# A decoder layer on one core: the order of the first loads, of the first two tiles' norms, and of the bias product

## The chip, the cores and the metric

The kernel runs on one core of one Trainium2 chip. The metric is the device time of that core for one execution, in microseconds (us). The engines are TensorE (PE; its weight loads are listed as PEld), VectorE (DVE), ScalarE (ACT), GpSimd (POOL) and SyncE (SP), whose queue issues nearly all transfers.

## The reference

One layer of a hybrid decoder, 512 positions by 1024 channels, float32:

```python
h = rms_norm(x, g_pre_mix)
q, k, v, xr, gr = split(h @ w_in)
attn = moba_attention(q, k, v, rel_bias)          # 8 heads of 64, blocks of 256, T5 bias
xr   = causal_dwconv(xr, w_conv_lru, b_conv_lru)  # width 4
lru  = rg_lru(xr, w_r, b_r, w_i, b_i, lam) * gelu(gr)
x    = x + rms_norm(concat(attn, lru) @ w_out, g_post_mix)
h    = rms_norm(x, g_pre_ffn)
c_u, c_g = split(causal_dwconv(h @ w_up, w_conv_ffn, b_conv_ffn))   # width 3, 2 x 2816
x    = x + rms_norm((gelu(c_g) * c_u) @ w_down, g_post_ffn)
```

## The kernel before

Positions are cut into four tiles of 128 rows. Every product of two float32 matrices is made from rounded parts: a high part (the value rounded to the PE's faster float32 form) and a low part (the rest), and three products high by high, low by high and high by low. So each operand is first copied by ScalarE (high) and then subtracted by VectorE or GpSimd (low).

The opening is written out by hand: from the first load to the end of the recurrent group's gates, PE, ScalarE, VectorE and SP each run in the order in which the lines stand (a block `manual_schedule`); behind it a planner orders the work, and POOL's order is the planner's throughout. What stands in the opening:

- Loads on SP: x tile 0 in two halves, x tile 1, then `load_xr(0)`, the first 128 columns of the weights for `xr` (512 KB, like a tile of x); then eight small loads of parameters into `rows` (L219 to L225); then x tile 2, `load_xr(1)`, x tile 3, `load_xr(2)`, `load_xr(3)` (L227 to L231), and four loads of the gate weights into `graw`. The scale of the norm, the one-hot table and the relative bias come on ScalarE's queue.
- Three warming products of PE (`keep_warm`, on constants, their result is not used), then `gpre`, the norm's scale spread over all rows by a product with ones, and `pfb` (L261), the product of the bias table with the one-hot table.
- Per tile of x: `sums` (ScalarE, squares with their sum), `rstd` (the root on ScalarE, some small operations on VectorE), `norm(t, half)` (VectorE), `turn(t, half)` (four PE transposes of 128 columns into one PSUM bank), `upper` (ScalarE copies the high part out) and `lower` (VectorE makes the low part).
- Per block of `xr` weights: `xr_upper(t)` (ScalarE's rounded copy) and `xr_lower(t, eng)` (the low part, on GpSimd for blocks 0 and 2, on VectorE for 1 and 3).
- `px_products(t, ...)`, the products of block t with half of the positions: C0 is the first two tiles, C1 the last two; 24 products each. The bank `p_x[t]` then goes to the conv (`conv_first` on ScalarE, `conv_rest` on VectorE), which needs `par`: the parameters in `rows`, transposed by two PE transposes into `ppar` and copied out by VectorE.
- Behind C1 come block 3 (`px3`), the gates (`gates(t)`, which read `xs`, the high and low part of the conv's result), the products for v and for g, and attention.
- `fb` is the scaled bias (L320, ScalarE, from `pfb`), stored to DRAM as `fbd` (L321), spread to `toep` by a transfer (L553) and read back by attention's `tb` loads.

PSUM banks are taken by tag: `mm` 3, `sc` 2, `tr` 2, `av` 1; a new tile of a tag waits for the readers of the one that had its bank.

Of the kernel before, what the change touches and what calls it, by code (L numbers as in the profile page):

```python
# [19 lines left out]
S = 512  # L20
D = 1024
H = 8
# [17 lines left out]
ISCALE = DH ** -0.5  # L40
# [12 lines left out]
def hybrid_layer(  # L53
# [6 lines left out]
    nc = tc.nc  # L60
# [9 lines left out]
    def bank(name, tag):  # L70
        return ps.tile([P, 512], F32, tag=tag, name=name, bufs=BANKS[tag])

    def f32(ap):
        return ap.bitcast(F32)


    def mm3(o, lhs, rhs, start, stop):
        (lh, ll), (rh, rl) = lhs, rhs
        nc.tensor.matmul(o, lh, rh, start=start, stop=False)  # L79
        nc.tensor.matmul(o, lh, rl, start=False, stop=False)  # L80
        nc.tensor.matmul(o, ll, rh, start=False, stop=stop)  # L81
# [5 lines left out]
    def load_raw(src, k, n):  # L87
        t = wp.tile([P, k, n], F32, tag="raw", name="raw", bufs=2)
        nc.sync.dma_start(t, src.rearrange("(k p) n -> p k n", p=P))
        return t  # L90
# [7 lines left out]
    def at(hl, *idx):  # L98
        return hl[0][idx], hl[1][idx]


    xres = cp.tile([P, NT, D], F32, name="xres")
    x_v = x.rearrange("(t p) d -> p t d", p=P)
# [7 lines left out]
    oh, rb = bias_in[:, :S], bias_in[:, S:S + H]  # L111
# [19 lines left out]
    def rstd_of(ss, first, name):  # L131


        v = cp.tile([P, 5], F32, tag="rs", name=name, bufs=8)
        nc.scalar.activation(v[:, 0:1], ss, AF.Sqrt, scale=1.0 / D, bias=first[:, 0:1])
        nc.vector.tensor_scalar(
            v[:, 1:2], ss, -0.5 / D, first[:, 1:2], op0=ALU.mult, op1=ALU.add)
        nc.vector.reciprocal(v[:, 2:3], v[:, 0:1])
        nc.vector.scalar_tensor_tensor(
            v[:, 3:4], v[:, 2:3], v[:, 1:2], v[:, 2:3], op0=ALU.mult, op1=ALU.mult)  # L140
        nc.vector.scalar_tensor_tensor(
            v[:, 4:5], v[:, 3:4], 1.5, v[:, 2:3], op0=ALU.add, op1=ALU.mult)
        return v[:, 4:5]
# [9 lines left out]
    def normalised(hn, t, r, gn, hs):  # L153
        nc.vector.scalar_tensor_tensor(
            hn[:, hs], xres[:, t, hs], r, gn, op0=ALU.mult, op1=ALU.mult)

    def transposes(hn, half, pt):
        for j in range(4):
            k = 4 * half + j
            nc.tensor.transpose(pt[:, j * P:(j + 1) * P], hn[:, k * P:(k + 1) * P], ident)  # L160

    def part(t, half):
        return slice(None), slice(4 * half, 4 * half + 4), slice(t * P, (t + 1) * P)

    def by_rows(pt):
        return pt.rearrange("p (k q) -> p k q", q=P)
# [31 lines left out]
    def xr_cols(t):  # L198
        return raw_xr[t // 2][:, :, (t % 2) * P:(t % 2 + 1) * P]

    def load_xr(t):
        nc.sync.dma_start(xr_cols(t), w_xr[:, :, t * P:(t + 1) * P])
# [8 lines left out]
    fb = gp.tile([H, FE], F32, name="fb")  # L211
# [4 lines left out]


    rows = pp.tile([P, 2, P], F32, name="rows")
    for r0, src in ((0, w_conv_lru[0]), (16, b_conv_lru), (20, b_r), (24, b_i), (28, lam)):  # L219
        v = src.rearrange("a (t c) -> (a t) c", c=P)  # L220
        nc.sync.dma_start(rows[r0:r0 + v.shape[0], 0], v)
# [1 line left out]
    wcf = w_conv_ffn[0].rearrange("a (t c) -> (a t) c", c=P)  # L223
    nc.sync.dma_start(rows[76:80, 0], wcf[P:P + 4])
    nc.sync.dma_start(rows[:, 1], wcf[0:P])  # L225

    nc.sync.dma_start(xres[:, 2], x_v[:, 2])  # L227
    load_xr(1)
    nc.sync.dma_start(xres[:, 3], x_v[:, 3])
    load_xr(2)  # L230
    load_xr(3)  # L231
    nc.gpsimd.memset(graw, 0.0)
    for g, w in enumerate((w_r[0], w_i[0])):
        wv = w.rearrange("(t b) c d -> b c t d", b=2)
# [6 lines left out]
    fbd = dp.tile([H, FE], F32, name="fbd")  # L241
# [7 lines left out]
    def keep_warm(n):  # L249

        for _ in range(n):
            nc.tensor.matmul(pwarm, warm[:, 0:P], warm, start=True, stop=True)
# [4 lines left out]
    gpre = [bank(f"gpre{n}", "sc") for n in range(2)]  # L257
    for n in range(2):
        nc.tensor.matmul(gpre[n], ones, g_row[:, n * 512:(n + 1) * 512], start=True, stop=True)
    pfb = bank("pfb", "av")  # L260
    nc.tensor.matmul(pfb[0:H, :], rb, oh, start=True, stop=True)  # L261


    hn, ssn, rn, pt = {}, {}, {}, {}
# [1 line left out]
    def sums(t, parts):  # L266
        hn[t] = pp.tile([P, D], F32, tag="hn", name="hn", bufs=4)
        ssn[t] = cp.tile([P, 4], F32, tag="ss", name="ss", bufs=8)
        square(t, ssn[t], parts, pp)

    def rstd(t, parts):
        ss = ssn[t]
        if parts == 2:
            for i, f in ((2, 1.0), (3, -0.5)):
                nc.vector.tensor_scalar(
                    ss[:, i:i + 1], ss[:, 0:1], f / D, f * EPS, op0=ALU.mult, op1=ALU.add)
            rn[t] = rstd_of(ss[:, 1:2], ss[:, 2:4], "rpre")
        else:
            rn[t] = rstd_of(ss[:, 0:1], consts, "rpre")

    def norm(t, half):
        normalised(hn[t], t, rn[t], gpre[half], slice(512 * half, 512 * half + 512))

    def turn(t, half, tag):
        pt[t, half] = bank("ptr", tag)
        transposes(hn[t], half, pt[t, half])

    def upper(t, half):
        nc.scalar.copy(hT[0][part(t, half)], by_rows(pt[t, half]))

    def lower(t, half):
        sl = part(t, half)
        nc.vector.tensor_sub(hT[1][sl], by_rows(pt[t, half]), f32(hT[0][sl]))
# [3 lines left out]
    def xr_upper(t):  # L297
        w_x[t] = [wp.tile([P, KD, P], F32R, tag=f"w{i}", name=f"w{i}") for i in "hl"]
        nc.scalar.copy(w_x[t][0], xr_cols(t))

    def xr_lower(t, eng):
        eng.tensor_sub(w_x[t][1], xr_cols(t), f32(w_x[t][0]))

    HH, HL, LH = range(3)
    BY_KIND = [(k, i) for i in (HH, HL, LH) for k in range(KD)]

    def px_products(t, c0, c1, todo, first, last):

        cs = slice(c0, c1)
        for n, (k, i) in enumerate(todo):  # L310
            nc.tensor.matmul(p_x[t][:, cs], w_x[t][i == LH][:, k], hT[i == HL][:, k, cs],  # L311
                             start=first and n == 0, stop=last and n == len(todo) - 1)

    C0, C1 = (0, S // 2), (S // 2, S)
    sums(0, 2)
    rstd(0, 2)
    sums(1, 1)
    norm(0, 0)
    rstd(1, 1)
    nc.scalar.mul(fb[:, 0:S], pfb[0:H, :], 1.0 / ISCALE)  # L320
    nc.sync.dma_start(fbd, fb)  # L321
    turn(0, 0, "tr")
    norm(1, 0)
    norm(0, 1)
    upper(0, 0)
    lower(0, 0)
    xr_upper(0)
    xr_lower(0, nc.gpsimd)
    turn(1, 0, "tr")
    upper(1, 0)  # L330
    turn(0, 1, "mm")
    upper(0, 1)
    norm(1, 1)
    lower(1, 0)
    lower(0, 1)
    p_x[0] = bank("px", "mm")
    px_products(0, *C0, [(k, HH) for k in range(4)], True, False)
    turn(1, 1, "av")
    upper(1, 1)
    lower(1, 1)  # L340
    px_products(0, *C0, [(k, HL) for k in range(4)] + [(k, HH) for k in range(4, 8)]
                + [(k, LH) for k in range(4)] + [(k, HL) for k in range(4, 8)]
                + [(k, LH) for k in range(4, 8)], False, True)
# [7 lines left out]
    px_products(1, *C0, BY_KIND, True, True)  # L351
    sums(3, 1)
    rstd(3, 1)
    turn(2, 0, "tr")
    turn(2, 1, "tr")
    upper(2, 0)
    upper(2, 1)
    norm(3, 0)
    norm(3, 1)
    xr_upper(2)  # L360
    xr_lower(2, nc.gpsimd)
    lower(2, 0)
    lower(2, 1)
    p_x[2] = bank("px", "mm")
# [4 lines left out]
    upper(3, 1)  # L369
    lower(3, 0)  # L370
    lower(3, 1)
    ppar = bank("ppar", "av")
    nc.tensor.transpose(ppar[:, 0:80], rows[0:80, 0], ident[0:80, 0:80])
    nc.tensor.transpose(ppar[:, 80:80 + P], rows[:, 1], ident)
    nc.vector.tensor_copy(par, ppar[:, 0:80 + P])
    for t in range(3):
        px_products(t, *C1, BY_KIND, True, True)
    xr_upper(3)
    xr_lower(3, nc.vector)

    def w_conv_l(tap, t):
        return par[:, 4 * tap + t:4 * tap + t + 1]
# [24 lines left out]
    av = lp.tile([P, NT, S], F32, name="av")  # L407
# [4 lines left out]
    def conv_first(t):  # L412
        nc.scalar.activation(xc[:, t], p_x[t], AF.Identity, scale=w_conv_l(3, t), bias=col(16 + t))

    def conv_rest(t):
        for d in range(1, 4):
            nc.vector.scalar_tensor_tensor(
                xc[:, t, d:], p_x[t][:, :S - d], w_conv_l(3 - d, t), xc[:, t, d:],
                op0=ALU.mult, op1=ALU.add)

    def xs_upper(t):
        xs[t] = [lp.tile([P, S], F32R, tag=f"xs{i}", name=f"xs{i}") for i in "hl"]
        nc.scalar.copy(xs[t][0], xc[:, t])
# [38 lines left out]
    def v_products(u, j):  # L462
        if u == 0 and j == 0:
            p_v.extend(bank(f"pv{t}", ("tr", "tr", "av", "mm")[t]) for t in range(NT))
        k = 2 * u + j
        for t in range(NT):
            mm3(p_v[t], at(hT, slice(None), k, slice(t * P, (t + 1) * P)),
                at(w_v[u], slice(None), j), k == 0, k == KD - 1)
# [11 lines left out]
    def gr_split(t):  # L480
        if t % 2 == 0:
            raw_gr.append(load_raw(w_in[:, GR0 + t * P:GR0 + t * P + 256], KD, 256))
        w_gr.append(split_w(raw_gr[-1][:, :, (t % 2) * P:(t % 2 + 1) * P], KD, P))
# [26 lines left out]
    nc.vector.tensor_sub(gw[1], graw, f32(gw[0]))  # L510
    conv_first(1)
    xs_upper(0)
    conv_rest(1)
    xs_lower(0)
    conv_first(2)
# [26 lines left out]
    gates(3)  # L542
    decay(2)
    gr_split(0)
    v_products(2, 1)
    sigmoids(3)
    gr_split(1)
# [349 lines left out]
```

## Time and profile before

| what | value |
|---|---|
| median of 3 runs | 589.23 us (588.77 to 589.48) |
| profiled execution, its own time | 588.1 us |
| its span, first to last instruction | 586.1 us |
| PE busy | 572.9 us (98%), 2731 products and transposes |
| PE weight loads | 472.4 us (81%) |
| VectorE, ScalarE, GpSimd busy | 358.4, 279.1, 15.5 us |
| transfers | 59.62 MB, mean 102 GB/s |

A product's row in the trace runs from its start to a modelled end, so rows of one engine overlap, and a full PE is not a PE at its peak. A row's last bracket gives the idle time of its engine just ahead of it and what ended that. Times are counted from the span's start.

### The profile page before, as it was taken

The numbers are of one execution on the slowest core, as the hardware profiler recorded it, in microseconds if no ns is written. First come the engines' busy times: TensorE is split into PE (matmuls) and PEld (weight loads), VectorE is DVE, ScalarE is ACT, GpSimd is POOL, SyncE is SP. The second block draws the span as 40 slices with busy tenths as digits, with TensorE's granted clock in tenths as the row PEclk, the third lists the DMA queues.
The fourth block names the chain that finished last, engine by engine and source line by source line (L and its number), as shares of the span: only waits on it lengthen the run. The fifth ranks groups of instructions, "written<-read, shape, count | busy, mean of one in ns | idle before, by whom it ended". The sixth has DMA issues, their size and how long they took to land.

```text
span 586.1 us, 7041 instructions
## 1 busy us (share of the span) xinstructions
PE 572.9 (98%) x2731; PEld 472.4 (81%) x2731; DVE 358.4 (61%) x649; ACT 279.1 (48%) x457; POOL 15.5 (3%) x37
## 2 busy tenths in 40 slices
PE   8899999999999999999999999999999999999995
PEld 4798888777778879988888888888888888888884
DVE  5687787898896895656656656656656521241225
ACT  6458856778775662534443443444444322132121
POOL 2150000000000000000000000000000000000000
PEclk9999999999999999999999999999999999999998
DMA  7824535333201614003413412412414223232103
GB/s 222 240 73 134 170 91 161 127 108 108 73 1 45 217 64 144 1 28 117 144 41 103 143 51 94 145 62 82 143 69 141 78 72 107 92 126 72 37 0 143
DMA packets 53449, 59.62 MB, mean 102 GB/s; under 512 B 2480, under 2 KB 42624, under 8 KB 53417
## 3 DMA queue, kind: packets, MB, share of 16 engines
q1 hardware_dynamic: 53319, 59.11, 31.3%
q8 instruction: 21, 0.34, 0.2%
q14 instruction: 11, 0.09, 0.1%
q10 hardware_dynamic: 98, 0.07, 0.0%
HBM read 57.06 MB, written 3.69 MB: 104 GB/s over the span
## 4 chain that ended last, share of the span: by engine, by line
PE 88%; DVE 4%; ACT 4%; DMA 2%; issue 1%; POOL 0%; SPq 0%; DVEq 0%; ACTq 0%
PE pup L80 14%; PE pup L81 14%; PE pup L79 14%; PE py L81 8%; PE py L79 8%; PE py L80 8%; PE px L311 2%; PE pq L79 2%; PE pq L80 2%; PE pq L81 2%; PE pav L661 2%; PE ptp L651 1%; PE pv L80 1%; PE pv L79 1%; PE pgr L80 1%; PE pgr L79 1%
## 5 line engine op out<-in xcount | busy, mean ns | idle before, releaser
L85 DVE TENSOR_TENSOR wl<-raw,wh 128x1024 fp32r<-128x1024 f32 x78 | 95.3, 1222 | 125.7 <-ACT wh L84 125.4
L84 ACT CAST wh<-raw 128x1024 fp32r<-128x1024 f32 x78 | 81.7, 1049 | 140.1 <-PE py L81 72.2
L81 PE MATMUL pup<-h2Th,wl 128*128 128x512 f32 x320 | 124.5, 389 | 0.0
L80 PE MATMUL pup<-h2Tl,wh 128*128 128x512 f32 x320 | 124.5, 389 | 0.0
L79 PE MATMUL pup<-h2Th,wh 128*128 128x512 f32 x320 | 124.3, 389 | 0.0
L81 PEld LDWEIGHTS pup<-h2Th,wl 128*128 128x128 f32 x320 | 60.1, 188 | 12.5
L80 PEld LDWEIGHTS pup<-h2Tl,wh 128*128 128x128 f32 x320 | 60.1, 188 | 12.5
L79 PEld LDWEIGHTS pup<-h2Th,wh 128*128 128x128 f32 x320 | 60.0, 188 | 12.3
L79 PE MATMUL py<-wh,acth 128*128 128x512 f32 x176 | 68.9, 391 | 0.0
L81 PE MATMUL py<-wh,actl 128*128 128x512 f32 x176 | 68.8, 391 | 0.0
L80 PE MATMUL py<-wl,acth 128*128 128x512 f32 x176 | 68.8, 391 | 0.0
L81 PEld LDWEIGHTS py<-wh,actl 128*128 128x128 f32 x176 | 33.1, 188 | 7.3
L80 PEld LDWEIGHTS py<-wl,acth 128*128 128x128 f32 x176 | 33.1, 188 | 7.2
L79 PEld LDWEIGHTS py<-wh,acth 128*128 128x128 f32 x176 | 33.1, 188 | 7.1
L819 DVE SCALAR_TENSOR_TENSOR yu<-pup,par,yu 128x511 f32<-128x511 f32 (+1 forms) x44 | 33.0, 749 | 4.3 <-ACT yu L817 3.6
L826 ACT ACTIVATE yg<-yg 128x512 f32<-128x512 f32 x22 | 13.9, 632 | 44.7 <-DVE yg L819 44.7
L819 DVE SCALAR_TENSOR_TENSOR yg<-pup,par,yg 128x511 f32<-128x511 f32 (+1 forms) x44 | 32.8, 746 | 2.0 <-ACT yg L817 1.2
L827 DVE TENSOR_TENSOR yu<-yu,yg 128x512 f32<-128x512 f32 x22 | 15.3, 693 | 18.0 <-ACT yg L826 18.0
L81 PE MATMUL py<-wh,mixTl 128*128 128x512 f32 x64 | 25.4, 397 | 0.0
L79 PE MATMUL pq<-hTh,wh 128*128 128x512 f32 x64 | 25.4, 396 | 0.0
L81 PE MATMUL pq<-hTh,wl 128*128 128x512 f32 x64 | 25.3, 396 | 0.0
L79 PE MATMUL py<-wh,mixTh 128*128 128x512 f32 x64 | 25.3, 395 | 0.0
(213 smaller groups left out, 934.4 us busy)
## 6 DMA issues: line engine op xcount, KB each, us to landing
raw<-in_w_up_dram SPq DMA_DIRECT2D x22, 1024.0 KB, 5.0
raw<-in_w_down_dram SPq DMA_DIRECT2D x10, 1024.0 KB, 5.0
raw<-in_w_in_dram SPq DMA_DIRECT2D x4, 1024.0 KB, 5.2
rawqk<-in_w_in_dram SPq DMA_DIRECT2D x8, 512.0 KB
raw<-in_w_out_dram SPq DMA_DIRECT2D x4, 1024.0 KB
raw<-in_w_in_dram SPq DMA_DIRECT2D x4, 512.0 KB
out_dram<-yz SPq DMA_DIRECT2D x8, 256.0 KB, 2.1
xres<-in_x_dram SPq DMA_DIRECT2D x3, 512.0 KB, 3.8
```

The costliest lines, as they stand in the source:

```text
L79: nc.tensor.matmul(o, lh, rh, start=start, stop=False)
L80: nc.tensor.matmul(o, lh, rl, start=False, stop=False)
L81: nc.tensor.matmul(o, ll, rh, start=False, stop=stop)
L84: nc.scalar.copy(h, src)
L85: (sub or nc.vector).tensor_sub(l, src, f32(h))
L311: nc.tensor.matmul(p_x[t][:, cs], w_x[t][i == LH][:, k], hT[i == HL][:, k, cs], start=first and n == 0, stop=last and n == len(todo) - 1)
L651: nc.tensor.transpose(ptr[:, j * P:(j + 1) * P], st[:, j * P:(j + 1) * P], ident)
L661: nc.tensor.matmul(pav[:, j * P:], vs, pT[i][:, j * S:j * (S - P) + S], start=j == 0 and i == 0, stop=j == NT - 1 and i == 1)
L819: nc.vector.scalar_tensor_tensor(y[:, d:], pt[:, :S - d], w_conv_f(2 - d, blk), y[:, d:], op0=ALU.mult, op1=ALU.add)
L826: nc.scalar.activation(yg, yg, AF.Gelu_apprx_tanh)
L827: nc.vector.tensor_mul(yu, yu, yg)
```

## The change

Parts of the opening change places; no arithmetic changes, and three warming products are added.

- SP: x tile 2, `load_xr(1)`, x tile 3, `load_xr(2)` and `load_xr(3)` go ahead of the eight loads of parameters. The store of `fb` moves behind `gr_split(0)`.
- PE: `pfb` leaves the start for a place between `px_products(1)` and `px_products(2)` of C1, and takes a bank of tag `sc`, where it had one of `av`; one warming product stands at its old place and two behind `turn(0, 0)`. The order is now turn(0,0), turn(0,1), turn(1,0), turn(1,1), then all of px(0) on C0 in one piece. The two parameter transposes go behind `px_products(0)` of C1.
- VectorE: both halves of tile 0's norm run one behind the other ahead of tile 1's `rstd`, then both of tile 1; the four `lower` of tiles 0 and 1 come behind them.
- ScalarE: `upper(0,0)`, `xr_upper(0)`, `upper(0,1)`, `upper(1,0)`, `upper(1,1)`; `xr_upper(2)` goes ahead of tile 2's `turn` and `upper`; the scaling of `fb` moves behind `xs_upper(0)`.

```diff
     rows = pp.tile([P, 2, P], F32, name="rows")
+    nc.sync.dma_start(xres[:, 2], x_v[:, 2])
+    load_xr(1)
+    nc.sync.dma_start(xres[:, 3], x_v[:, 3])
+    load_xr(2)
+    load_xr(3)
     for r0, src in ((0, w_conv_lru[0]), (16, b_conv_lru), (20, b_r), (24, b_i), (28, lam)):
...
-    nc.sync.dma_start(xres[:, 2], x_v[:, 2])
-    load_xr(1)
-    nc.sync.dma_start(xres[:, 3], x_v[:, 3])
-    load_xr(2)
-    load_xr(3)
...
-    pfb = bank("pfb", "av")
-    nc.tensor.matmul(pfb[0:H, :], rb, oh, start=True, stop=True)
+    keep_warm(1)
...
     norm(0, 0)
+    norm(0, 1)
     rstd(1, 1)
-    nc.scalar.mul(fb[:, 0:S], pfb[0:H, :], 1.0 / ISCALE)
-    nc.sync.dma_start(fbd, fb)
     turn(0, 0, "tr")
-    norm(1, 0)
-    norm(0, 1)
+    keep_warm(2)
     upper(0, 0)
-    lower(0, 0)
     xr_upper(0)
     xr_lower(0, nc.gpsimd)
+    turn(0, 1, "mm")
+    upper(0, 1)
+    norm(1, 0)
+    norm(1, 1)
     turn(1, 0, "tr")
     upper(1, 0)
-    turn(0, 1, "mm")
-    upper(0, 1)
-    norm(1, 1)
+    turn(1, 1, "av")
+    upper(1, 1)
+    lower(0, 0)
     lower(1, 0)
     lower(0, 1)
+    lower(1, 1)
     p_x[0] = bank("px", "mm")
     px_products(0, *C0, [(k, HH) for k in range(4)], True, False)
-    turn(1, 1, "av")
-    upper(1, 1)
-    lower(1, 1)
...
     rstd(3, 1)
+    xr_upper(2)
+    xr_lower(2, nc.gpsimd)
     turn(2, 0, "tr")
...
     norm(3, 1)
-    xr_upper(2)
-    xr_lower(2, nc.gpsimd)
...
     lower(3, 1)
+    px_products(0, *C1, BY_KIND, True, True)
     ppar = bank("ppar", "av")
...
-    for t in range(3):
-        px_products(t, *C1, BY_KIND, True, True)
+    px_products(1, *C1, BY_KIND, True, True)
+    pfb = bank("pfb", "sc")
+    nc.tensor.matmul(pfb[0:H, :], rb, oh, start=True, stop=True)
+    px_products(2, *C1, BY_KIND, True, True)
...
     xs_upper(0)
+    nc.scalar.mul(fb[:, 0:S], pfb[0:H, :], 1.0 / ISCALE)
...
     gr_split(0)
+    nc.sync.dma_start(fbd, fb)
```

## Rows read from the trace of the kernel before

**Rows 1.** Busy time by stretch: engine busy (instructions), granted clock, DMA share, GB/s.

```profile
0.00:27.00 27.00, 22.89 (x115) 15.49 (x115) 14.47 (x37) 14.68 (x28) 6.51 (x10) 1.00 0.85 251
27.00:100.00 73.00, 72.96 (x355) 61.76 (x356) 57.23 (x76) 49.45 (x70) 9.01 (x27) 1.00 0.39 115
100.00:250.00 150.00, 147.46 (x814) 123.41 (x814) 120.05 (x322) 97.83 (x203) 0.00 (x0) 1.00 0.28 92
```

**Rows 2.** Chain of waits, opening: start, us, what.

```profile
1.63 5.06 DMA xres<-in_x_dram
...
22.26 2.41 POOL wl L302
```

**Rows 3.** Timeline of PE's weight loads, 13 to 28 us: start, us, what, idle before.

```profile
18.47 1.02 PEld L311 LDWEIGHTS px<-hTh,wl 128*128 128x128 f32 x8 [0.32 <-DVE wl L302]
...
22.23 1.00 PEld L311 LDWEIGHTS px<-hTh,wh 128*128 128x128 f32 x8 [1.91 <-ACT wh L299]
...
24.71 1.02 PEld L311 LDWEIGHTS px<-hTh,wl 128*128 128x128 f32 x8 [0.51 <-POOL wl L302]
25.67 0.90 PEld L160 LDWEIGHTS ptr<-ident,hn 128*128 128x128 f32 x8
26.53 0.14 PEld L373 LDWEIGHTS ppar<-ident,rows 80*128 80x128 f32 x1
...
27.04 1.02 PEld L311 LDWEIGHTS px<-hTh,wh 128*128 128x128 f32 x8 [0.26 <-ACT hTh L289]
```

**Rows 4.** Timeline of all engines, first 14 us.

```profile
1.51 1.46 PE L252 MATMUL pwarm<-warm 128*128 128x512 bf16 x3 [1.51 <-DVE warm L246]
...
4.60 0.63 ACT L150 ACTIVATE sqn<-xres 128x512 bf16<-128x512 f32 x1 [0.38 <-DMA xres<-in_x_dram]
...
6.40 0.75 DVE L154 SCALAR_TENSOR_TENSOR hn<-xres,rpre,gpre 128x512 f32<-128x512 f32 x1
...
6.60 1.87 PE L261 MATMUL pfb<-bias_in 32*8 32x512 f32 x2
...
6.71 1.06 ACT L150 ACTIVATE sqn<-xres 128x1024 bf16<-128x1024 f32 x1 [1.06 <-DMA xres<-in_x_dram]
...
7.89 0.29 ACT L135 ACTIVATE rpre<-ss,consts 128x1 f32<-128x1 f32 x1
7.89 0.21 DVE L136 TENSOR_SCALAR rpre<-ss,consts 128x1 f32<-128x1 f32 x1 [0.75 <-ACT sqn L150]
...
8.40 1.11 PE L160 MATMUL ptr<-ident,hn 128*128 128x128 f32 x4
...
8.87 1.41 DVE L154 SCALAR_TENSOR_TENSOR hn<-xres,rpre,gpre 128x512 f32<-128x512 f32 x2
...
10.04 1.05 ACT L299 CAST wh<-raw 128x1024 fp32r<-128x1024 f32 x1
...
13.23 0.59 ACT L289 CAST hTh<-ptr 128x512 fp32r<-128x512 f32 x1 [0.97 <-PE ptr L160]
```

**Rows 5.** Timeline of SP's queue, first 14 us.

```profile
8.41 0.36 SPq L225 DMA_DIRECT2D rows<-in_w_conv_ffn_dram  x1
...
12.95 3.31 SPq L236 DMA_DIRECT2D graw<-in_w_r_dram  x1
```

**Rows 6.** DMA issues: what, KB each, us from issue to landing.

```profile
rows<-in_w_conv_lru_dram SPq DMA_DIRECT2D x1, 8.0 KB, 6.0
```

**Rows 7.** Timeline of VectorE, 27 to 39 us.

```profile
28.23 0.36 DVE L375 COPY par<-ppar 128x208 f32<-128x208 f32 x1
...
31.04 2.32 DVE L417 SCALAR_TENSOR_TENSOR xc<-px,par,xc 128x511 f32<-128x511 f32 x3 [0.96 <-ACT xc L413]
...
34.09 1.25 DVE L510 TENSOR_TENSOR gwl<-graw,gwh 128x1024 fp32r<-128x1024 f32 x1 [0.45 <-issue]
...
37.48 0.68 DVE L426 TENSOR_TENSOR xsl<-xc,xsh 128x512 fp32r<-128x512 f32 x1
```

**Rows 8.** Timeline of PE, 38 to 39.5 us.

```profile
38.76 0.39 PE L80 MATMUL pg<-xsl,gwh 128*128 128x512 f32 x1
```

## The prediction

> **What bounds the kernel now.** I read the busy time by stretch first, then the chain of waits, then the timelines of the first 40 us. The stretches [rows 1] show a matrix engine (PE) that is busy 72.96 of the 73 us from 27 to 100 and 147.46 of the 150 from 100 to 250. From 27 us on its own work sets the end. Before 27 us its busy time is 22.89 us, but rows that stand one behind another with waits in them, and rows at half the pace, count in it in full. So only two things can move the time: the moment at which PE becomes continuous, which is the first product on the second half of the columns (px C1, 27.04 us, whose row comes below), and PE work added after that moment. The chain [rows 2] starts with the landing of x tile 1 (issued 1.63, 5.06 us), ends this opening with the GpSimd remainder of weight block 2 (22.26, 2.41 us) and in between passes from ScalarE to VectorE to PE and back.
>
> Two facts of the opening matter. In PE's weight loads [rows 3] there are two waits late in it: 1.91 us until 22.23 for ScalarE's rounded copy of weight block 2 (it stands behind the four eviction halves of tile 2), and 0.51 us until 24.71 for GpSimd's remainder of the same block, which can start only after that copy. And in the first 14 us [rows 4] PE takes pfb, the bias product, from 6.60 to 8.47, while the first normalised half of tile 0 is ready at 6.40 + 0.75 = 7.15; its transposes start only at 8.40. The granted clock reads 1.00 in all of 0 to 27 [rows 1], yet these rows show the lower of the two levels, 1.2 GHz: four transposes take 1.11 us at 8.40 [rows 4], while the weight loads of eight take 0.90 at 25.67 [rows 3], the pace of the other level, 2.4 GHz. The rows of the timeline double their pace near 12.5, after transposes and first products since 8.40.
>
> **The change, part by part.** All sums are against the profiled execution, 588.1 us (span 586.1); the median of the runs is 589.23, 1.1 above, and I carry the gain over to it.
>
> *Opening of tiles 0 and 1.* pfb leaves: PE does one warming product instead. Three took 1.46 us [rows 4], so 0.49: PE is free at 6.60 + 0.49 = 7.1, and turn(0,0) starts at 7.2 instead of 8.40. At the lower clock it takes 1.11 us, to 8.35. ScalarE has finished tile 1's root at 7.89 + 0.29 = 8.18, so upper(0,0) runs 8.37 to 8.96 and the copy of weight block 0 (1.05 us [rows 4]) 8.97 to 10.03, against 10.04 to 11.09 before. The scaling of fb is gone from this spot; it cost nothing before, since the transposes that ScalarE needs next ended at 9.5. norm(0,1) is moved up to 7.15 to 7.88, into VectorE's 0.75 us of idle time before 7.89 [rows 4]; tile 1's chain of small operations then starts on time and its two halves run 8.87 to 10.3. It costs nothing; if tile 1 landed earlier it would cost up to 0.73. On PE: two warming products to 9.3, turn(0,1) to 10.3, turn(1,0) and turn(1,1) 1.0 each at the lower clock, 0.45 each at the higher. ScalarE's last three evictions follow. With the lower clock to the end they finish at about 12.85, with the higher one from 10.3 on at 11.9 (three evictions at 0.55 behind 10.3). Before, the last one ended at 13.23 + 0.59 = 13.82 [rows 4]. I take the middle, since PE is busy from 6.6 on instead of 8.40 without pfb's narrow product in it: 12.4, a gain of **1.4** (0.95 to 1.9). Tile 2's squares, its root and the copy of weight block 1 stand behind that eviction and move with it. All four low parts now follow the norms on VectorE; the last ends at about 13.6, 0.1 to 0.2 late for tile 2's small operations, within the spread. Weight block 0's remainder on GpSimd (2.4 us) starts near 10.1 and ends by 12.5, before its turn in px(0).
>
> *Weight block 2 ahead of tile 2's evictions.* Weight block 1's remainder frees PE at 18.47 [rows 3], by the above at 17.1. Then come 8 products, turn(2,*) and px(2). ScalarE reaches the copy of block 2 right after tile 3's root: two sums of squares (6.71 to 7.89 [rows 4]: 1.18), two roots (0.29) and a copy (1.05) are 4.0 us behind 12.4, so it runs 16.4 to 17.45, and GpSimd's 2.4 us end at 19.9. PE wants the copy at 17.1 + 0.96 + 0.90 = 19.0 (eight products, 24.71 to 25.67, and eight transposes [rows 3]) and the remainder 16 products later, at 20.9. Both waits go: 1.91 + 0.51 = **2.4 us** [rows 3]. The evictions of tile 2 now come after the copy, near 18.6, and nobody needs them before px C1. Next late is tile 3's own path (8 transposes 0.90, one eviction 0.60, then 27.04), as now. PE becomes continuous at 27.04 - 1.4 - 2.4 = 23.2.
>
> *Added behind that point.* pfb stands now between px(1) and px(2) of the second half. Its 1.87 us [rows 4] were at the lower clock, so 0.93 at the higher; four f32 transposes of 128 columns, about 0.45 [rows 3], are the same number of columns for one of its two passes, which gives 0.9. The two transposes of the parameters ran from 26.53 [rows 3] inside the 0.26 us wait before 27.04 and the eviction's time; now they lie in the full stretch: 0.2. Together **1.1 us** lost, with no cover.
>
> *VectorE behind it.* par is copied only once px(0) of C1 has run, 3.3 us behind the start of the stretch instead of 28.23 - 27.04 = 1.2. From that copy to the low part of xs the trace needs 38.16 - 28.23 = 9.93 us, with idle gaps of 0.96 and 0.45 in it [rows 7]. The gate product that reads it runs 38.76 - 27.04 = 11.7 behind the start [rows 8], now 12.8 since 1.1 us of work is ahead of it. With both gaps it would be late by 0.4; the first gap was a wait for ScalarE's conv_first, which now finds its px finished, so 3.3 + 8.97 = 12.3 is in time. I take 0, bound 0.4. fb's scaling lands where ScalarE waits for px(2): 0.
>
> *The queues.* Eight parameter loads, 0.1 MB, go behind five loads of 512 KB on SP's queue. x tile 2 is issued near 2.6 instead of 8.8, and they follow block 0 (8.41 [rows 5]) without a pause. At 1.7 to 2.1 us for each 512 KB (8.41 - 6.71; 6.71 - 4.60 [rows 4]) tile 2 lands at 10.1 to 10.5, block 1 at 12.6, tile 3 at 14.7, block 2 at 16.8 at the latest; ScalarE wants them at 12.4, 13.9, 14.9 and 16.4. Only the last can be 0.4 late, inside the 1.0 that the copy of block 2 has to spare on PE: 0. The bias store leaves SP's early part and stands behind the first g weights, which wait for v's products; the Toeplitz copy that reads it stands behind the same weights now, and attention reads that much later: free. The four gate loads stay behind all of these; their reader on ScalarE stands behind conv_first(0), near 29, and they come up under (c).
>
> Sum: 1.4 + 2.4 - 1.1 = 2.7. Profiled 588.1 - 2.7 = 585.4, median **586.5**.
>
> **A rule against it.** x tile 1 landed 2.1 us behind tile 0 (ScalarE's waits end at 4.60 and 6.71 [rows 4]) with 512 KB queued behind it, weight block 0 1.7 us later (SP's wait for it ends at 8.41 [rows 5]) with little behind it; so a full queue costs a load 0.4 here, and block 0 at 8.8 is still in time for 8.97. The Trainium skill (DMA: Bandwidth & Descriptors, section Latency and other measured facts) puts HBM's access latency at 0.2 us on average and 2 us at high load. By that, an estimate, tile 1 could land up to 1.8 us later, and the time would be 588.3. The trace bears out only the small end.
>
> **The rivals.** (a) *The opening brings nothing*: x tile 1 and weight block 0 land later as x tile 2 and more weights are read behind them, by as much as pfb's leaving gives, 1.4 us. For: the landing of tile 1 heads the chain [rows 2]. Against: the 0.4 above. Then 2.4 - 1.1 = 1.3 is left: 587.9. (b) *Given back later*: PE idles 2.54 us of 100 to 250 [rows 1], where a planner orders the work; its order may come out otherwise, or VectorE is late for the gates by the 0.4 and for what follows. With 1.5 given back: 588.0. (c) *Parameters late, slower*: PE works in order, so a parameter load that has not landed when PE reaches the two transposes, at 23.2 + 2.9 = 26.1, stops px(1) and all behind it, 1 us for each us; from 28.8 on the gain is gone, and at 30 the kernel is measurably slower. For: one issue on SP already took 3.31 us [rows 5], and the loads now wait for the big ones. Against: the bytes ahead are those that stand ahead of the gate loads now, the first of which is through its issue at 12.95 + 3.31 = 16.3; the longest landing of such a load is 6.0 [rows 6], which gives 22.3. The gate loads come after that with 29 to meet. Price if it hits, a landing at 30: 3.9, less the 2.7, is 1.2 above 589.23: 590.4.
>
> **Chances.** Forecast 0.66 (its own range 585.4 to 587.4: gains of 1.8 to 3.8 by the bounds of the clock, the landings and VectorE). (a) 0.13, (b) 0.11, (c) 0.07, better than all this 0.03. The range 585.2 to 588.4 holds the forecast, most of (a) and most of (b). A measurement tells about 0.2%, 1.2 us, from no change: faster means under 588.05. The forecast, the better case and half of (a) and (b) are under it: 0.66 + 0.03 + 0.12 = 0.81; the other half of (a) and (b) is the same, 0.12; slower is (c), 0.07.
>
> **What would show it.** Right: px C1 starts near 23.2; the weight loads of px(2) show no wait for ScalarE or GpSimd; turn(0,0) starts near 7.2; transposes at the higher pace before 12.5; two pfb rows of about 0.45 between px rows; PE full from there on. Wrong: a first sum of squares of tile 1 later than 7.1 (a); PE idle before the parameter transposes (c); PE idle before the first gates or more than 2.5 us of it from 100 to 250 (b); px C1 later than 25.

## The result, and the profile after

| | before | changed |
|---|---|---|
| median | 589.19 us (588.77 to 589.48) | 585.99 us (585.59 to 586.61) |
| ratio | | 0.9947, 95% interval 0.993 to 0.9964 |
| profiled execution, its span | 588.1, 586.1 us | 586.3, 584.2 us |

The changed kernel is faster by 3.1 us, by the ratio; beside the later experiments it stood once more at 0.9954 (0.9941 to 0.9968), 2.7 us. The forecast was 586.5, in a range of 585.2 to 588.4.

PE's weight loads of the changed kernel from 13 to 32 us, to be held against [rows 3] (start, us, what, idle before):

```profile
18.08 1.01 PEld L309 LDWEIGHTS px<-hTh,wl 128*128 128x128 f32 x8
19.04 0.90 PEld L160 LDWEIGHTS ptr<-ident,hn 128*128 128x128 f32 x8
19.91 1.01 PEld L309 LDWEIGHTS px<-hTh,wh 128*128 128x128 f32 x8
20.85 1.03 PEld L309 LDWEIGHTS px<-hTl,wh 128*128 128x128 f32 x8
21.80 1.03 PEld L309 LDWEIGHTS px<-hTh,wl 128*128 128x128 f32 x8
...
23.45 0.42 PEld L160 LDWEIGHTS ptr<-ident,hn 128*128 128x128 f32 x4 [0.18 <-DVE hTl L291]
24.18 1.14 PEld L309 LDWEIGHTS px<-hTh,wh 128*128 128x128 f32 x8 [0.32 <-ACT hTh L287]
...
27.18 0.14 PEld L371 LDWEIGHTS ppar<-ident,rows 80*128 80x128 f32 x1
...
30.43 0.09 PEld L376 LDWEIGHTS pfb<-bias_in 32*8 32x8 f32 x2
```

Both late waits of [rows 3] are gone: px(2) follows the transposes of tile 2 at 19.91 and its low part at 21.80 without a bracket. px C1 starts at 24.18, 2.86 earlier than 27.04, though not at the forecast 23.2. From there on PE is full, as the busy time by stretch shows, and what it idles later is as before (147.46 of 150 in [rows 1]):

```profile
27.00:100.00 73.00, 73.00 (x346) 60.72 (x345) 56.86 (x75) 49.67 (x71) 9.45 (x27) 1.00 0.43 133
100.00:250.00 150.00, 147.59 (x817) 123.79 (x816) 119.61 (x321) 97.08 (x203) 0.00 (x0) 1.00 0.28 89
```

Behind px C1 stand the added products. The product behind all of px(0) to px(2), px3, starts 10.18 us after px C1 (34.36 - 24.18), where it started 8.74 us after it before (35.78 - 27.04). PE's products in the changed kernel, and below them px3 before:

```profile
29.38 1.12 PE L309 MATMUL px<-hTh,wl 128*128 128x256 f32 x8
30.43 1.02 PE L376 MATMUL pfb<-bias_in 32*8 32x512 f32 x2
31.38 1.22 PE L309 MATMUL px<-hTh,wh 128*128 128x256 f32 x8
...
34.36 0.40 PE L79 MATMUL px<-hTh,wh 128*128 128x512 f32 x1
```
```profile
35.78 0.40 PE L79 MATMUL px<-hTh,wh 128*128 128x512 f32 x1
```

ScalarE in the first 14 us, against [rows 4]: tile 0's second half is there at 5.61 (4.60 before), tile 1 at 7.81 (6.71), and still the last eviction ends at 13.43 instead of 13.82.

```profile
5.61 0.63 ACT L150 ACTIVATE sqn<-xres 128x512 bf16<-128x512 f32 x1 [1.39 <-DMA xres<-in_x_dram]
...
7.81 1.06 ACT L150 ACTIVATE sqn<-xres 128x1024 bf16<-128x1024 f32 x1 [1.15 <-DMA xres<-in_x_dram]
...
9.42 0.59 ACT L287 CAST hTh<-ptr 128x512 fp32r<-128x512 f32 x1
9.90 1.05 ACT L297 CAST wh<-raw 128x1024 fp32r<-128x1024 f32 x1
...
12.84 0.59 ACT L287 CAST hTh<-ptr 128x512 fp32r<-128x512 f32 x1 [0.27 <-PE ptr L160]
13.32 1.06 ACT L150 ACTIVATE sqn<-xres 128x1024 bf16<-128x1024 f32 x1
```

So this profile shows 0.4 us of the 1.4 forecast for the opening. Its first transposes, turn(0,0), wait for VectorE's norm until 8.30:

```profile
8.30 1.09 PE L160 MATMUL ptr<-ident,hn 128*128 128x128 f32 x4 [1.09 <-DVE hn L154]
```

VectorE and, from its own timeline, GpSimd near 18 us. A small operation on 128 by 1 elements takes 2.30 us, as long as GpSimd's remainder of weight block 2 beside it. Before, the same operation took 0.22 (second fence). No step of the prediction has this.

```profile
18.26 2.30 DVE L139 SCALAR_TENSOR_TENSOR rpre<-rpre 128x1 f32<-128x1 f32 x1
20.59 0.16 DVE L141 SCALAR_TENSOR_TENSOR rpre<-rpre 128x1 f32<-128x1 f32 x1
20.79 1.41 DVE L154 SCALAR_TENSOR_TENSOR hn<-xres,rpre,gpre 128x512 f32<-128x512 f32 x2
```
```profile
18.64 0.22 DVE L139 SCALAR_TENSOR_TENSOR rpre<-rpre 128x1 f32<-128x1 f32 x1
```
```profile
18.14 2.39 POOL L300 TENSOR_TENSOR wl<-raw,wh 128x1024 fp32r<-128x1024 f32 x1 [4.74 <-ACT wh L297]
```

### The profile page after: what moved, and what is told of

Read it like the earlier page. It is cut to its first block, busy times and chain, and to the rows that moved or that the text cites. A ratio compares the mean times of both kernels' runs of the same rounds, so it can differ in the third digit from the quotient of the medians.

```text
span 584.2 us, 7051 instructions
## 1 busy us (share of the span) xinstructions
PE 572.6 (98%) x2734; PEld 473.5 (81%) x2734; DVE 360.3 (62%) x649; ACT 279.7 (48%) x457; POOL 15.9 (3%) x37
## 4 chain that ended last, share of the span: by engine, by line
PE 91%; DVE 4%; ACT 3%; DMA 1%; issue 1%; DVEq 0%; SPq 0%; ACTq 0%
PE pup L80 14%; PE pup L81 14%; PE pup L79 14%; PE py L81 8%; PE py L80 8%; PE py L79 8%; PE px L309 3%; PE pq L79 2%; PE pq L80 2%; PE pq L81 2%; PE pav L663 2%; PE ptp L653 1%; PE pgr L80 1%; PE pgr L79 1%; PE pv L80 1%; PE pv L79 1%
## 5 line engine op out<-in xcount | busy, mean ns | idle before, releaser
L80 PEld LDWEIGHTS pup<-h2Tl,wh 128*128 128x128 f32 x320 | 60.1, 188 | 12.5
L79 PEld LDWEIGHTS pup<-h2Th,wh 128*128 128x128 f32 x320 | 60.0, 188 | 12.5
```

## The experiments

Each was timed in five rounds (e2 in eleven) against the kernel before on its own chip, whose median there was 588.54, 588.22 and 588.50 in the three groups; so ratios are compared, with their 95% intervals.

### Parts alone, and parts undone

**e1, weight block 2 alone.**

```diff
     rstd(3, 1)
+    xr_upper(2)
+    xr_lower(2, nc.gpsimd)
...
     norm(3, 1)
-    xr_upper(2)
-    xr_lower(2, nc.gpsimd)
```

> The kernel before with one part of the change alone: weight block 2's rounded copy and its GpSimd remainder ahead of tile 2's turns and evictions. Theory (the prediction's second term): both late waits of PE in the opening go, 1.91 + 0.51 us, nothing is added, px C1 starts near 24.6 instead of 27.04; 589.2 - 2.4 = 586.8. Rival (the waits are covered, tile 3's path is late next): px C1 stays within 0.5 us of 27.04 and the time at 588.7 or more.

Measured: 0.9958 (0.9944 to 0.9971), 586.1 us, 2.5 us less. PE's weight loads in its timeline:

```profile
18.99 1.02 PEld L311 LDWEIGHTS px<-hTh,wl 128*128 128x128 f32 x8 [0.31 <-DVE wl L302]
19.95 0.90 PEld L160 LDWEIGHTS ptr<-ident,hn 128*128 128x128 f32 x8
...
24.80 0.14 PEld L373 LDWEIGHTS ppar<-ident,rows 80*128 80x128 f32 x1
```

From 18.99 to the parameter transposes are 5.81 us, where [rows 3] has 26.53 - 18.47 = 8.06: the two waits, 2.25. px C1 starts at 25.14; the theory's 24.6 is missed by the opening, which was 0.5 us later in this profile (tile 2's squares at 14.23, before 13.71). This one move is nearly the whole gain of the change.

**e2, the load order alone** (the kernel before with the five big loads first).

> The kernel before with the load order alone: x tiles 2 and 3 and weight blocks 1 to 3 ahead of the eight parameter loads. In the changed kernel's profile tile 0's second half landed at 5.61 and tile 1 at 7.81, against 4.60 and 6.71 before. Theory Q (the loads queued behind slow those ahead): here too they land about 1.0 later, and the chain of the opening moves with them: 590.2. Rival N (it was the spread between executions): they land at 4.6 and 6.7, and since nothing in the opening before waits for tile 2, the time stays at 589.2.

Measured: 0.9996 (0.9987 to 1.0004). In its one profile tile 1 landed at 6.74, and both waits of PE stand where they were:

```profile
21.85 1.01 PEld L311 LDWEIGHTS px<-hTh,wh 128*128 128x128 f32 x8 [1.91 <-ACT wh L299]
...
24.31 1.01 PEld L311 LDWEIGHTS px<-hTh,wl 128*128 128x128 f32 x8 [0.48 <-POOL wl L302]
```

Without the other parts nothing waits for the loads that are brought forward. The 1.0 us that theory Q adds to the time does not come. Whether the queue slows tile 1 can't be told from one profile; see below.

**e3, five small loads first** (the changed kernel).

```diff
+    for r0, src in ((0, w_conv_lru[0]), (16, b_conv_lru), (20, b_r), (24, b_i), (28, lam)):
+        ...
     nc.sync.dma_start(xres[:, 2], x_v[:, 2])
     load_xr(1)
```

> The changed kernel with five of the eight parameter loads put back ahead of x tile 2, so that tile 2 is issued near 5 us instead of 2.6; all else as changed. Theory Q: tile 1 lands near 6.8 again, tile 2 near 10.3, and what stands behind them moves up by 0.9: 586.0 - 0.9 = 585.1. Rival N: tile 1 lands as in the changed kernel in its common execution and the time stays at 586.0.

Measured: 0.995 (0.9938 to 0.9963), no different from the changed kernel; tile 1 landed at 7.09. Theory Q's 585.1 would be a ratio of 0.9931, outside the interval.

**e4, the bias product back at the start** (the changed kernel).

```diff
-    keep_warm(1)
+    pfb = bank("pfb", "mm")
+    nc.tensor.matmul(pfb[0:H, :], rb, oh, start=True, stop=True)
...
     px_products(1, *C1, BY_KIND, True, True)
-    pfb = bank("pfb", "sc")
-    nc.tensor.matmul(pfb[0:H, :], rb, oh, start=True, stop=True)
...
```

> The changed kernel with the bias product back at its old place (in a bank of tag mm) in place of one warming product, and its scaling back on ScalarE ahead of the first eviction. Theory: with tile 1 landing at 7.8 its root ends at 9.3, so the first transposes have time to start at 8.5 instead of 8.3; the opening loses 0.2 and the full stretch is shorter by pfb's 0.9: 586.0 - 0.7 = 585.3. Rival (the prediction's first term: pfb in the start holds up the transposes by 1.2): 586.0 - 0.9 + 1.2 = 586.3.

Measured: 0.9962 (0.995 to 0.9975), 586.0: no gain. The stretch was shorter, but PE now idled in it, 0.36 us from 27 to 100, and its waits name VectorE's low part of xs before the gates (columns of the second: who waited for whom, us in total, times, longest):

```profile
27.00:100.00 73.00, 72.64 (x346) 60.65 (x346) 56.65 (x75) 48.90 (x70) 9.45 (x27) 1.00 0.42 130
```
```profile
PEld pg L80 <- DVE xsl L426: 0.6, 1, 0.6
```

That is the prediction's rival (b) in small, at its bound of 0.4: par comes late, because its transposes stand behind px(0), and in the changed kernel it was pfb that covered this. The opening of this profile was late too: tile 2's squares start at 13.74, later than in any of the five profiles of the new opening without pfb at the start (table below), and pfb itself waited 0.27 us for its operands.

### Spread, warming, and VectorE's long small operation

**a1, the changed kernel again.**

> The changed kernel once more, unaltered, beside the next three on one chip: its ratio to the kernel before, 0.9947 (586.0) in the first comparison. If the landing of tile 1 (7.81 in its first profile) and the moment at which PE's rows double their pace (near 13.4) belong to the change, both come again here; if they are the spread between executions, tile 1 lands between 6.7 and 7.8 and the pace doubles anywhere from 12 to 13.5.

Measured: 0.9954 (0.9941 to 0.9968). Tile 1 landed at 7.81 once more, but PE's pace doubled earlier than either theory has it. The transposes of this profile, and below them those of the first:

```profile
9.51 1.06 PE L160 MATMUL ptr<-ident,hn 128*128 128x128 f32 x4
10.77 1.38 PE L160 MATMUL ptr<-ident,hn 128*128 128x128 f32 x8 [0.20 <-DVE hn L154]
12.10 0.73 PE L309 MATMUL px<-hTh,wh 128*128 128x256 f32 x4
```
```profile
10.03 2.77 PE L160 MATMUL ptr<-ident,hn 128*128 128x128 f32 x12
12.62 1.22 PE L309 MATMUL px<-hTh,wh 128*128 128x256 f32 x4
```

In the second the four products at 12.62 still take 1.22 us, in the first those at 12.10 take 0.73. Row by row, transposes or products that follow one another start 0.21 us apart up to 10.2 in a1 and up to 13.9 in the first profile, and 0.11 to 0.12 apart from 10.9 and 14.0 on: the same kernel, the same granted clock of 1.00 in the busy time by stretch, and a change of pace 3 us apart. So that moment does not belong to the change.

**e5, no added warming products.**

```diff
-    keep_warm(1)
...
-    keep_warm(2)
```

> The changed kernel without its three added warming products. Theory W (they do not lift the clock in time: in the profile PE stays at the lower pace until 13.4 with them): the two behind the first transposes only hold PE up for 0.9 us, and the last eviction of tile 1 comes about 0.3 earlier: 585.7. Theory C (the prediction: they bring the higher clock forward): without them the pace doubles later and the time is 0.5 to 1.0 longer: 586.5 to 587.0.

Measured: 0.9957 (0.9945 to 0.997). The time decides between neither theory: it is 0.35 us above a1 by the medians, inside the intervals. In its one profile PE was at the lower pace until 15.6, later than in any other, but by a1 against the first profile one such moment proves nothing. Tile 2's squares started at 12.86 all the same, as in the other profiles of this opening.

**e7, the small operations with one tensor input.**

```diff
+        if name == "rone":
+            nc.vector.tensor_scalar(
+                v[:, 3:4], v[:, 2:3], v[:, 1:2], v[:, 2:3], op0=ALU.mult, op1=ALU.mult)
+            nc.vector.tensor_scalar(
+                v[:, 4:5], v[:, 3:4], 1.5, v[:, 2:3], op0=ALU.add, op1=ALU.mult)
+            return v[:, 4:5]
         nc.vector.scalar_tensor_tensor(
...
-            rn[t] = rstd_of(ss[:, 0:1], consts, "rpre")
+            rn[t] = rstd_of(ss[:, 0:1], consts, "rone")
```

> The changed kernel with the last two small VectorE operations of rstd for tiles 1 to 3 written with one tensor input and the others as per-partition scalars (same arithmetic). In the changed kernel's profile one of them, on 128 by 1 elements, takes 2.30 us, 0.1 us after GpSimd's remainder of weight block 2 started and as long as that runs. Theory L (two tensor inputs of VectorE wait for GpSimd's operation): each of them now takes 0.2 us, tile 3's norms start near 18.8 instead of 20.8, the 0.18 us wait of tile 3's second transposes goes and px C1 starts 0.2 to 0.3 earlier: 585.7. Rival (the wait has another cause, the semaphore or the order): the operation stays at 2.3 us.

Measured: 0.9954 (0.9941 to 0.9966), equal to a1. The mechanism is as theory L has it: GpSimd runs from 17.55 for 2.39 us, and both operations take their short time in the midst of it; tile 3's norms start at 18.34.

```profile
17.78 0.27 DVE L140 TENSOR_SCALAR rone<-rone 128x1 f32<-128x1 f32 x1
18.09 0.21 DVE L142 TENSOR_SCALAR rone<-rone 128x1 f32<-128x1 f32 x1
18.34 1.41 DVE L160 SCALAR_TENSOR_TENSOR hn<-xres,rone,gpre 128x512 f32<-128x512 f32 x2
```
```profile
17.55 2.39 POOL L306 TENSOR_TENSOR wl<-raw,wh 128x1024 fp32r<-128x1024 f32 x1 [4.72 <-ACT wh L303]
```

But nothing that counts was waiting: the norms are due at PE near 22.3, and 2 us earlier buys nothing. The 0.18 us wait of tile 3's second transposes went, as theory L has it, but px C1 started at 23.69, between the 23.50 and 24.18 of the two profiles of the changed kernel.

### A version that beats both

**e6, bias product and parameters ahead of the full stretch**: e3 and e4 together, and the parameter transposes ahead of px(0) of C1.

```diff
+    ppar = bank("ppar", "av")
+    ...
     px_products(0, *C1, BY_KIND, True, True)
-    ppar = bank("ppar", "av")
-    ...
```

> The changed kernel with the bias product at its old place, the parameter transposes ahead of px(0) of C1 as before, and five of the parameter loads ahead of x tile 2. Both products leave the full stretch (pfb measured 1.04 there, the transposes 0.2 to 0.3), the first transposes of tile 0 start up to 0.8 later, and par is ready earlier, so that PE's 0.36 us idle time before the gates, which appeared with pfb at the start, does not come: 586.0 - 1.3 + 0.8 = 585.5. Rival (the opening is worth more than the stretch): 586.5 or more.

Measured: 0.9937 (0.9924 to 0.9949), 584.5 us. PE is full from 27 to 100 again (73.00 of 73), and px3 starts 8.81 us after px C1, as before the change. Against e4, at 0.9962, two things differ: with par early the idle time before the gates and the 0.2 us of the transposes in the stretch go, 0.6 in all; and the opening of this profile is 0.8 us earlier (tile 2's squares at 12.93 for 13.74), with five of the small loads first. What each is worth was not tried apart.

The last group put four kernels on one chip.

> The kernel before with weight block 2 ahead alone, once more, so that the next three stand beside it on one chip. By the first comparison 0.9958 of before, 2.5 us less.

> The changed kernel with the bias product and the parameter transposes ahead of the full stretch and five parameter loads first, once more beside the others. By the earlier comparison 0.9937. If the opening's new order is worth what the profiles of the unchanged and the changed opening show (tile 2's squares start at 13.3 to 14.2 with the old order, at 12.7 to 13.3 with the new, means 13.75 and 12.9), it is 0.9 us below the kernel with block 2 alone: 0.9943; if nothing of that order reaches the end, the two are equal.

> The same without the two warming products behind the first transposes. Theory C (they bring the higher pace forward): 0.3 to 1.0 us more than with them. Theory W (they only stand in the way): 0.3 less.

> The kernel before with weight block 2 ahead and the new load order, old opening. With block 2 ahead ScalarE waited 0.16 us for that block's load in its profile, so the load order, worth nothing alone, should now give about 0.2 us: 0.9955. Rival: it changes nothing, 0.9958, since PE wants the copy 1 us later than ScalarE makes it.

| kernel | median, us | ratio to before | 95% interval |
|---|---|---|---|
| b1, block 2 alone, again | 586.06 | 0.9957 | 0.9943 to 0.9971 |
| e9, block 2 and load order, old opening | 585.90 | 0.9957 | 0.9944 to 0.997 |
| b6, e6 again | 584.78 | 0.9939 | 0.9925 to 0.9953 |
| e8, e6 without the two warming products | 583.93 | 0.9925 | 0.9912 to 0.9938 |

The load order adds nothing to block 2 either; the wait of 0.16 us is gone in e9, but it had cover, since in e1 the copy ends at 19.24 and PE comes to it at 20.84. b6 is 1.3 us below b1 by the medians, and the five executions of the one (583.92 to 584.90) all lie below those of the other (585.36 to 586.38): the new opening, taken whole, reaches the end. e8 is the fastest, 4.4 us below the kernel before. Its 16 transposes of tiles 0 and 1 run in one piece, and the products behind them are at the higher pace:

```profile
8.41 3.67 PE L160 MATMUL ptr<-ident,hn 128*128 128x128 f32 x16
12.12 0.74 PE L310 MATMUL px<-hTh,wh 128*128 128x256 f32 x4
```

Theory C is not borne out here. That the warming products stand in the way is not shown either: against b6 the intervals overlap, tile 2's squares start alike in the two profiles (12.60 and 12.63), and e5 against a1 has no such gain.

**All profiles together.** When ScalarE began with tile 1 (its landing) and with tile 2's squares (the end of the opening for tiles 0 and 1), in us, one profile each:

| loads behind weight block 0 | tile 1 | mean |
|---|---|---|
| parameters (before, e1, b1) | 6.71, 6.96, 6.93 | 6.87 |
| five small, then the big ones (e3, e6, b6, e8) | 7.09, 6.94, 6.27, 7.08 | 6.85 |
| the big ones (changed, a1, e2, e4, e5, e7, e9) | 7.81, 7.81, 6.74, 7.45, 7.41, 7.17, 7.22 | 7.37 |

| opening | tile 2's squares | mean |
|---|---|---|
| old (before, e1, e2, b1, e9) | 13.71, 14.23, 13.32, 14.27, 14.57 | 14.02 |
| new, pfb in the stretch (changed, a1, e3, e5, e7) | 13.32, 12.66, 12.83, 12.86, 12.74 | 12.88 |
| new, pfb at the start (e4, e6, b6, e8) | 13.74, 12.93, 12.63, 12.60 | 12.98 |

Six of the seven with the big loads right behind are later than all seven others: the landing that theory Q of e2 expects is there after all, at 0.5 us in the mean with a spread as large, but its price in time showed in neither e2 nor e3. e2's own profile was the seventh.

The old opening's squares follow the moment at which PE's pace doubles: 13.32 with 11.6 (e2), 13.71 with 12.5 (before), 14.57 with 15.4 (e9). The new one's hardly do: 12.66 with 10.9 (a1), 12.86 with 15.6 (e5); its two above 13 are those in which tile 0's second half landed last (changed 5.61, e4 5.36). So the gain of the opening is no fixed figure: at like moments single profiles differ by 0.4 us (e2, e6, both near 11.5) to 1.7 us (e9, e5).

## Why the prediction was right, step by step

- **Weight block 2** (2.4 us): right in place and size, 2.5 and 2.5 us in e1 and b1. It is the gain.
- **Opening of tiles 0 and 1** (1.4 us, 0.95 to 1.9): 14.02 - 12.88 = 1.1 by the means of the profiles. The direction held, by other steps than told. The step "pfb leaves, so turn(0,0) starts at 7.2" failed: the transposes started at 8.30 and 7.78 (a1), since tile 0's second half landed at 5.61 and 5.09; and with pfb back at the start, in e6, b6 and e8, tile 2's squares come as early as without it (12.93, 12.63, 12.60; e3, with the same loads, 12.83). So pfb's leaving gave the opening nothing that the profiles show, and that the sum came near is luck. So is the middle taken for the clock, as the pace doubled by 10.9 in a1 and at 13.9 in the first profile. What remains is the order: four turns in one piece, without the first products in between. The order as a whole is shown, in e6, b6 and e8; its single moves were not tried apart.
- **pfb and the parameter transposes in the full stretch** (1.1 us): a little under-sized, 1.3. From px C1 to px3 the changed kernel takes 1.44 us longer, but 0.1 of that comes from a late second eviction of tile 3, which e1 has too, without the added work (8.86 there). The five profiles with both in the stretch have 10.06 to 10.18 us, the eight with both ahead of it 8.74 to 8.86, and e4, with the transposes alone in it, 9.03. pfb holds PE for 1.04 (the last group of px(1) begins at 29.38 and takes 0.96, px(2) begins at 31.38), the group behind it starts 0.1 slower, and the transposes take 0.2.
- **VectorE behind it** (0, bound 0.4): 0 in the changed kernel, 0.36 in e4, where pfb no longer covered it. The bound was the right one.
- **The queues**: the last parameter load was issued at 17.49 and its transposes ran at 27.18 without a wait; rival (c) did not come. Rival (a) came in part: the big loads cost tile 1 about 0.5 us, near the 0.4 of the rows. Its sign, tile 1 later than 7.1, stood in both profiles of the changed kernel (7.81), but its price did not: in the first the opening still gave 0.4 us, in a1 1.05. The figure of the Trainium skill (DMA: Bandwidth & Descriptors, Latency and other measured facts), by which, as an estimate, it could have been 1.8, is not reached: the largest was 1.1.
- **The sum.** 2.5 + 1.1 - 1.3 = 2.3 by the rows, against 3.1 and 2.7 measured, with intervals of about 1 us either way: the rest is inside them. All of it lies ahead of px3: from px3's start to the end of the profiled execution are 551.5 to 552.4 us in thirteen of the fourteen profiles, and 552.9 in e4, which idles before the gates. px3 starts at 35.78 before, at 34.36 and 33.67 in the changed kernel, at 34.00 and 34.06 with block 2 alone, and at 32.63, 32.33 and 32.28 in e6, b6 and e8. The profiled execution alone (1.8 less) would have misled, since its tile 1 was among the latest and its pace doubled late, while the one before was 1.1 us below its own median.
- **Not foreseen**: VectorE's 2.30 us beside GpSimd. The Trainium skill has the rule (SBUF — State Buffer, section SBUF: two separate sides): VectorE and GpSimd share a pair of ports, and a VectorE operation with two SBUF inputs and a GpSimd operation that reads SBUF exclude each other for a whole instruction. The trace agrees, 2.30 against 0.22, and e7 shows it by the operand alone. It would have changed no number here, because even the late norms end at 22.20, ahead of the transposes that read them (22.85).

Of the change's parts, then, the move of two lines for weight block 2 gives 2.5; the new opening gives about 1.1, and pfb and the parameters in the full stretch take about 1.3 back. So the last two cancel, and the changed kernel (0.9947, 0.9954) is not told apart from block 2 alone (0.9958, 0.9957). e6 and e8 keep the first two without the third.

## What to carry to other kernels

Where an engine is full from some moment on, a wait just ahead of that moment is worth its whole length, and work moved behind it costs its whole length: small products belong into the gaps of the opening, where pfb cost nothing that the profiles of e6, b6 and e8 show. A move that only pays with another (par's transposes with pfb) shows nothing or a loss when it is tried alone. With a spread of 1 us between executions of one kernel, one profile of each side is no measure of a 2 us change; several openings laid side by side are, and the start of the first product behind all that was moved (px3 here) sums them up in one number.

## What the runs showed of the hardware

- PE's rows ran at half pace for the first 10.9 to 15.6 us of the fourteen profiles, with the granted clock at 1.00 throughout. The moment of the change lay 3 us apart in two executions of the same kernel (10.9 and 13.9), and three added products showed no effect that the time could tell.
- A single issue can hold up the engine that makes it for microseconds. In all seven profiles with the five 512 KB loads right behind weight block 0, SP took 3.0 to 3.7 us to issue x tile 3; in the other seven it took under 0.6. The changed kernel, and below it the kernel before:

```profile
4.28 3.61 SPq L221 DMA_DIRECT2D xres<-in_x_dram  x1
```
```profile
9.76 0.58 SPq L229 DMA_DIRECT2D xres<-in_x_dram  x1
```

- A VectorE operation on 128 by 1 elements with two tensor inputs took 2.30 us beside GpSimd's remainder of weight block 2, and 0.22 without it; written with one (e7) it took 0.27 beside it.
- A landing in the opening has a spread of 0.8 to 1.1 us between profiles with the same load order (x tile 1: 6.27 to 7.09, and 6.74 to 7.81), as large as most of the terms of the sum.
